# Elementwise products of a state-space table builder and a head norm from GpSimd to VectorE, and 1 / rms applied by ScalarE behind the rotary step

## The chip, the cores and the metric

The kernel runs on one core of one Trainium2 chip. The time is the device time of one execution in microseconds (us). The engines work side by side, each on its own queue of instructions in a fixed order: TensorE (PE in the rows; PEld is its weight load), VectorE (DVE), ScalarE (ACT), GpSimd (POOL) and SyncE (SP), which here only issues transfers. An instruction that waits holds up all that stand behind it on its engine.

## The reference, cut to what matters

One step of a hybrid decoder layer for a prompt of 512 tokens and for 8 single tokens that continue cached sequences. One input projection feeds a diagonal state-space group (S5) and an attention group with three branches; both are gated, concatenated and projected out. The change touches two pieces of it, the norm with rotary step of the heads, and the discretised tables of the state-space group:

```python
def rms_norm(x, w):
    y = xf * lax.rsqrt(jnp.mean(xf * xf, axis=-1, keepdims=True) + RMS_EPS)
    return (y * w).astype(x.dtype)

def rope(x, pos):                     # first 16 of 64 columns of a head
    return concatenate([x1 * cos - x2 * sin, x2 * cos + x1 * sin, rest], axis=-1)

q = rope(rms_norm(q.reshape(B, S, 8, 64), q_norm_w), pos)
ks = rope(rms_norm(kv[:, :, 0::2], k_norm_w), pos)      # 3 branches x 2 heads of keys

# s5_scan: h[t] = a * h[t-1] + B u[t], y = Re(C h) + D u, with a = exp(lam dt) complex
```

## The kernel before

All products of the dense projections are made as three TensorE passes (L121 to L123: high by high, high by low, low by high), so every weight block is split on the way in: ScalarE copies the high part (`whi`), VectorE subtracts it (`wlo`).

The program up to about 205 us of the trace merges two streams. `dense` makes the projections, block of 256 columns by block: keys and values, queries (tile `qraw`, evacuated from TensorE's accumulator `a` by ScalarE), then the four gate blocks (`gate_mm`, tile `sg`, evacuated by VectorE as `sg<-a` and by ScalarE as `sgS<-a`). `ssm_all` works the 32 state-space groups in four rounds `sq` of eight: `ssm_tables(sq)` builds the tables `P` (turned by TensorE and copied by ScalarE to `WX`), `WY`, `E` and the kernel `ktc`; `ssm_run(sq)` makes `Xc` on TensorE, turns it with `E` into `ga`, scans it on VectorE (`ga<-coef,ga`), and multiplies the result `HB` with `WY` (L782) and the input with `TT` (L787); ScalarE copies the sum out as `ga<-t`. `coef`, one buffer, is written by ScalarE for each scan and waits for the scan before.

`norm_rope(i, keys)` runs between the dense blocks for the four tiles of 128 prompt rows and for the 8 sample rows (`kvs`, `qsr`), once for keys and once for queries: ScalarE squares into `sq` (two buffers, shared), GpSimd multiplies the norm weight in, VectorE reduces (`rsq<-sq`) and scales, GpSimd raises to -1/2 (L168), VectorE multiplies 1 / rms in and does the rotary step (`ra`, `rb`, then back into the tile). Finished keys go out by SP's queue. Behind 205 us lie prompt attention, the gathered cache of the sample rows, the gated unit and the output projection.

The order of each engine's queue is made when the program is built, by a scheduler that walks the recorded program with estimated durations; reads from PSUM get a higher priority. So a change of engine also moves other instructions. The two calls that the change moves about are

```python
def rstd_of(out, ssq, n, parts, cols):
    V.tensor_scalar(out, ssq, 1.0 / n, EPS, op0=ALU.mult, op1=ALU.add)
    return G.tensor_tensor(out, out, mhalf[:parts, :cols], op=ALU.pow)
```

and, in `norm_rope`, the product of the whole tile with `rb`. L61 and L62 are the wrapper through which all VectorE and ScalarE calls go, so those rows are told apart by their tiles.

Of the kernel before, what the change touches and what calls it, by code (L numbers as in the profile page):

```python
# [13 lines left out]
ALU = mybir.AluOpType  # L14
# [22 lines left out]
def hymba_step_kernel(  # L37
# [9 lines left out]
    G, T = nc.gpsimd, nc.tensor  # L47
# [18 lines left out]
    V, S = PsumFirst(nc.vector), PsumFirst(nc.scalar)  # L66
# [16 lines left out]
    def pt_(name, cols=1024, dt=F32, parts=128):  # L83
        return big.tile([parts, cols], dt, tag="P", name=nm(name), bufs=NP)
# [7 lines left out]
    def st(shape, name, dt=F32, bufs=1, tag=None):  # L92
        n = nm(name)
        return sm.tile(shape, dt, tag=tag or n, name=n, bufs=bufs)

    def k2(name, cols=512, parts=128, dt=F32):
        return sm.tile([parts, cols], dt, tag="k2", name=nm(name), bufs=NK)
# [4 lines left out]
    def k1(name, cols=128, parts=128, dt=F32):  # L102
        return sm.tile([parts, cols], dt, tag="k1", name=nm(name), bufs=NS)
# [6 lines left out]
    def pb(use):  # L110
        tag = ROUTE[use]
        return psum.tile([128, 512], F32, tag=tag, name=nm(tag), bufs=BANKS[tag])
# [53 lines left out]
# [3 lines that stand above are left out]
# [102 lines left out]
    rs = st([8, 1], "rs")  # L271
# [172 lines left out]
    def rowset(i):  # L444
        if i < 4:
            return 128, kvt[i], qraw[i // 2][:, 512 * (i % 2):512 * (i % 2) + 512]
        return 8, kvs, qsr
# [63 lines left out]
    def part_of(n, w):  # L511
        j = 0 if so[0] + n * w <= HW else 1
        o = so[j]
        so[j] += n * w
        return ssm[j][:, o:o + n * w].rearrange("p (a b) -> p a b", b=w)
# [92 lines left out]
    pwr, pwi, pni = part_of(9, 16), part_of(9, 16), st([128, 9, 16], "pni", tag="pni")  # L608
# [15 lines left out]
    CTr, CTi, CNi = part_of(16, 16), part_of(16, 16), st([128, 16, 16], "CNi", tag="CNi")  # L624
# [14 lines left out]
    bbr, bbi = part_of(16, 16), part_of(16, 16)  # L639
# [28 lines left out]
    def ssm_tables(sq):  # L668

        gs = slice(4 * sq, 4 * sq + 4)  # L670
        P_ = pt_("P")
        Pr, Pi, pt1, pt2 = P_[:, 0:512], P_[:, 512:1024], k2("pt"), k2("pt")

        def v4(t):
            return t.rearrange("p (g s c) -> p g s c", s=8, c=16)

        def pw4(t, e0):
            return t[:, e0:e0 + 8, gs].rearrange("p e g -> p g e").unsqueeze(3).to_broadcast([128, 4, 8, 16])

        def c4(t):  # L680
            return t[:, gs].unsqueeze(2).to_broadcast([128, 4, 8, 16])

        V.tensor_tensor(v4(pt1), pw4(pwr, 1), c4(bbr), op=ALU.mult)
        G.tensor_tensor(v4(pt2), pw4(pni, 1), c4(bbi), op=ALU.mult)
        V.tensor_tensor(Pr, pt1, pt2, op=ALU.add)
        V.tensor_tensor(v4(pt1), pw4(pwr, 1), c4(bbi), op=ALU.mult)
        G.tensor_tensor(v4(pt2), pw4(pwi, 1), c4(bbr), op=ALU.mult)
        V.tensor_tensor(Pi, pt1, pt2, op=ALU.add)
        for g2 in range(2):
            sl = slice(64 * g2, 64 * g2 + 64)  # L690
            S.copy(cb[sl, 0, :, g2, :], CTr[sl, gs])
            S.copy(cb[sl, 1, :, g2, :], CNi[sl, gs])
        WX = pt_("WX")
        for a in range(2):
            p = pb("tr")
            for b in range(4):
                T.transpose(p[:, 128 * b:128 * b + 128], P_[:, 512 * a + 128 * b:512 * a + 128 * b + 128], ident)
            S.copy(WX[:, 512 * a:512 * a + 512], p)
        p = pb("tr")
        for a in range(2):  # L700
            for gp in range(4):
                T.matmul(p[32 * gp:32 * gp + 32, 0:128], cb[:, a, gp].rearrange("p a c -> p (a c)"),
                         P_[:, 512 * a + 128 * gp:512 * a + 128 * gp + 128], start=(a == 0), stop=(a == 1),
                         skip_group_check=True, tile_position=(0, 32 * gp))
        ktt = k1("ktt")
        S.copy(ktt, p[:, 0:128])
        p = pb("tr")
        T.transpose(p[:, 0:128], ktt, ident)

        ktc = k1("ktc")  # L710
        k3_ = ktc.rearrange("p (c g) -> p g c", g=8)
        S.copy(k3_, p[:, :128].rearrange("p (g c) -> p g c", c=16))
        V.tensor_tensor(k3_[96:128], k3_[96:128], Dm[96:128, 128 * sq:128 * sq + 128].rearrange("p (g c) -> p g c", c=16),
                        op=ALU.add)
        nc.sync.dma_start(scr_k[sq, 0:128, :], ktc)

        WY = pt_("WY")
        w1_, w2_ = k2("wt"), k2("wt")
        V.tensor_tensor(v4(w1_), pw4(pwr, 0), c4(CTr), op=ALU.mult)
        G.tensor_tensor(v4(w2_), pw4(pni, 0), c4(CTi), op=ALU.mult)  # L720
        V.tensor_tensor(WY[:, 0:512], w1_, w2_, op=ALU.add)
        V.tensor_tensor(v4(w1_), pw4(pni, 0), c4(CTr), op=ALU.mult)
        G.tensor_tensor(v4(w2_), pw4(pwr, 0), c4(CNi), op=ALU.mult)
        V.tensor_tensor(WY[:, 512:1024], w1_, w2_, op=ALU.add)

        E = k2("E").rearrange("p (a g k) -> p a g k", a=2, k=64)
        for a in range(2):
            S.copy(E[:, a, :, 0:32], UW[a][:, gs, 0:32])
        es = k2("es").rearrange("p (b a g k) -> p b a g k", b=2, a=2, k=32)
        for b in range(2):  # L730
            V.tensor_tensor(es[:, b], E[:, :, :, 0:32], UW[b][:, gs, 32:33].unsqueeze(1).to_broadcast([128, 2, 4, 32]), op=ALU.mult)
        V.tensor_tensor(E[:, 0, :, 32:64], es[:, 0, 0], es[:, 1, 1], op=ALU.subtract)
        V.tensor_tensor(E[:, 1, :, 32:64], es[:, 0, 1], es[:, 1, 0], op=ALU.add)
        return WX, WY, E
# [85 lines left out]
    def norm_rope(i, keys):  # L820

        n, kv_, q_ = rowset(i)
        if keys:
            src = kv_.rearrange("p (k v n) -> p k v n", v=2, n=128)[:, :, 0, :]
            hd, h, sh = src.rearrange("p k (g d) -> p k g d", g=2), 6, (n, 3, 2)
            nw_ = nw4[:n, 1:4].unsqueeze(2).to_broadcast([n, 3, 2, 64])
            e = lambda t: t.rearrange("p (k g) d -> p k g d", g=2)
            bc = lambda t: t.unsqueeze(1).unsqueeze(1).to_broadcast([n, 3, 2, 8])
        else:
            src = q_  # L830
            hd, h, sh = src.rearrange("p (h d) -> p h d", d=64), 8, (n, 8)
            nw_ = nw4[:n, 0:1].to_broadcast([n, 8, 64])
            e = lambda t: t
            bc = lambda t: t.unsqueeze(1).to_broadcast([n, 8, 8])
        sq = k3("sq", 64 * h, n)
        S.activation(sq.rearrange("p (k n) -> p k n", n=128) if keys else sq, src, AF.Square)
        G.tensor_tensor(hd, hd, nw_, op=ALU.mult)
        rs = st([n, 14], "rsq", bufs=2, tag=f"rsq{n}")[:, 0:h]
        V.tensor_reduce(rs, sq.rearrange("p (h d) -> p h d", d=64), axis=AX.X, op=ALU.add)
        o = C_ROPE + 16 * i if i < 4 else C_ROPS  # L840
        cos, sin = bc(cst[:n, o:o + 8]), bc(cst[:n, o + 8:o + 16])
        x1, x2 = hd[..., 0:8], hd[..., 8:16]
        rstd_of(rs, rs, 64, n, h)
        rb = e(rs.unsqueeze(2)) if keys else rs.unsqueeze(2)
        V.tensor_tensor(hd, hd, rb.to_broadcast([*sh, 64]), op=ALU.mult)
        ra, rb_ = k1("ra", 128, n), k1("rb", 128, n)
        r_ = [e(t[:, 8 * h * j:8 * h * j + 8 * h].rearrange("p (h d) -> p h d", d=8)) for t in (ra, rb_) for j in range(2)]
        for out, x, cs_ in zip(r_, (x1, x2, x2, x1), (cos, sin, cos, sin)):
            V.tensor_tensor(out, x, cs_, op=ALU.mult)
        V.tensor_tensor(x1, r_[0], r_[1], op=ALU.subtract)  # L850
        last["nr"] = V.tensor_tensor(x2, r_[2], r_[3], op=ALU.add)
        if not keys:
            return
        if i < 4:
            nc.sync.dma_start(kvp_rows[128 * i:128 * i + 128], kv_[:, 0:512])
            nc.sync.dma_start(winp_rows[128 * i:128 * i + 128], kv_[:, 512:768])
        else:
            nc.sync.dma_start(kv_sample[0, :, 0].rearrange("b k g d -> b (k g d)"), kvs[:, 0:512])
            nc.sync.dma_start(win_sample[0, :, 511].rearrange("b k g d -> b (k g d)"), kvs[:, 512:768])
# [49 lines left out]
    def dense():  # L909
# [19 lines left out]
        for i in (4, 0, 1):  # L929
            norm_rope(i, True)  # L930
# [816 lines left out]
```

## Time and profile before

| | before |
|---|---|
| median of 3 runs | 485.32 us (484.53 to 486.43) |
| the profiled execution | 485.31 us |
| its span in the trace | 483.4 us |
| TensorE busy | 456.5 us, 94% of the span |
| VectorE busy | 353.8 us, 73% |
| ScalarE busy | 241.1 us, 50% |
| GpSimd busy | 124.8 us, 26% |

The span is the stretch from the first to the last instruction in the trace; the time has 1.9 us more around it. Busy shares are means over stages that differ. Matmuls overlap in the rows, so a busy TensorE is one that has something in flight.

### The profile page before, as it was taken

How to read it: one execution, taken by the hardware profiler on the slowest of the kernel's cores; microseconds unless marked ns; L12 is line 12 of the kernel's file. 1: busy time of each engine (PE TensorE's matmuls, PEld its weight loads, DVE VectorE, ACT ScalarE, POOL GpSimd, SP SyncE). 2: the span in 40 equal slices, each digit the busy share in tenths (PEclk: the TensorE clock that was granted, in tenths of full speed). 3: DMA queues.
4: the chain of work that ended last, by engine and by line, in shares of the span. 5: the costliest groups of instructions: out<-in, count | busy, mean ns of one | idle time of the engine just before them, and what ended most of it. 6: DMA issues, size and time to landing. Idle time of an engine off the chain costs nothing.

```text
span 483.4 us, 10948 instructions
## 1 busy us (share of the span) xinstructions
PE 456.5 (94%) x4258; PEld 387.9 (80%) x4258; DVE 353.8 (73%) x914; ACT 241.1 (50%) x585; POOL 124.8 (26%) x130
## 2 busy tenths in 40 slices
PE   7999999889698999979999999999999899999997
PEld 4989998688697898979867866777667599899886
DVE  6978999999998974648485875868557667774332
ACT  5914755545234222656675667747565636442100
POOL 3100045489673000063244213421324010000000
PEclk8999999899899999989999999999999899999999
DMA  8776622335256182065433272337244974612211
GB/s 285 234 218 169 112 52 89 92 91 115 48 144 191 51 195 39 1 216 177 133 102 117 88 263 88 129 122 241 92 161 132 261 179 132 173 35 77 66 45 46
DMA packets 75603, 62.84 MB, mean 130 GB/s; under 512 B 29230, under 2 KB 69024, under 8 KB 75424
## 3 DMA queue, kind: packets, MB, share of 16 engines
q1 hardware_dynamic: 66176, 36.74, 27.8%
q0 software_dynamic: 4816, 17.03, 10.7%
q10 hardware_dynamic: 4560, 8.39, 5.6%
q8 instruction: 33, 0.54, 0.5%
q14 instruction: 18, 0.15, 0.1%
HBM read 55.63 MB, written 10.70 MB: 137 GB/s over the span
## 4 chain that ended last, share of the span: by engine, by line
PE 65%; DVE 19%; issue 8%; DMA 5%; ACT 2%; POOL 1%; SPq 0%; DVEq 0%; POOLq 0%; ACTq 0%
PE a L121 9%; PE a L122 9%; PE a L123 9%; PE ph L1362 8%; PE a L1252 4%; PE a L1216 4%; PE t L1243 3%; DVE wlo L62 3%; PE t L1338 3%; DVE ga L62 3%; PE c L1535 2%; DMA kvg<-in_cache_kv_dram,idx 2%; PE t L1328 2%; DVE rsq L62 1%; DMA x<-in_x_prompt_dram 1%
## 5 line engine op out<-in xcount | busy, mean ns | idle before, releaser
L121 PE MATMUL a<-hTh,whi 128*128 128x256 f32 (+1 forms) x192 | 55.6, 291 | 7.3 <-ACT qraw L61 4.4
L122 PE MATMUL a<-hTh,wlo 128*128 128x256 f32 (+1 forms) x192 | 55.4, 290 | 0.0
L1319 POOL DMA_INDIRECT kvg<-in_cache_kv_dram,idx x32 | 31.9, 998 | 89.0 <-PE c L1119 56.1
L123 PE MATMUL a<-hTl,whi 128*128 128x256 f32 (+1 forms) x192 | 53.9, 287 | 0.0
L123 PE MATMUL a<-wlo,hTh 128*128 128x256 f32 (+1 forms) x160 | 46.6, 292 | 2.3 <-DVE wlo L62 2.3
L121 PE MATMUL a<-whi,hTh 128*128 128x256 f32 (+1 forms) x160 | 46.3, 293 | 0.0
L122 PE MATMUL a<-whi,hTl 128*128 128x256 f32 (+1 forms) x160 | 46.1, 289 | 0.0
L1362 PE MATMUL ph<-XT,W1h 128*128 128x256 f32 x256 | 44.7, 298 | 0.2 <-ACT XT L61 0.2
L121 PEld LDWEIGHTS a<-hTh,whi 128*128 128x128 f32 x192 | 36.9, 192 | 8.7 <-ACT qraw L61 4.6
L61 ACT ACTIVATE P<-a,mx 128x128 f32<-128x128 f32 (+3 forms) x64 | 33.6, 533 | 13.4 <-DVE mx L61 12.1
L61 DVE TENSOR_REDUCE mx<-a 128x1 f32<-128x384 f32 (+3 forms) x48 | 28.0, 596 | 13.5 <-PE a L1217 13.4
L122 PEld LDWEIGHTS a<-hTh,wlo 128*128 128x128 f32 x192 | 36.9, 192 | 0.6 <-issue 0.4
L123 PEld LDWEIGHTS a<-hTl,whi 128*128 128x128 f32 x192 | 36.4, 192 | 0.0
L121 PE MATMUL a<-woh,mixh 128*128 128x256 f32 x128 | 36.2, 285 | 0.0
L123 PE MATMUL a<-wol,mixh 128*128 128x256 f32 x128 | 36.1, 284 | 0.0
L122 PE MATMUL a<-woh,mixl 128*128 128x256 f32 x128 | 35.8, 282 | 0.0
L1362 PEld LDWEIGHTS ph<-XT,W1h 128*128 128x128 f32 x256 | 34.8, 190 | 1.0 <-ACT XT L61 0.6
L123 PEld LDWEIGHTS a<-wlo,hTh 128*128 128x128 f32 x160 | 31.0, 194 | 2.9 <-DVE wlo L62 2.5
L1322 POOL COPY Vs<-kvg 128x256 f32<-128x256 f32 x32 | 14.5, 454 | 70.2 <-DMA kvg<-in_cache_kv_dram,idx 47.7
L121 PEld LDWEIGHTS a<-whi,hTh 128*128 128x128 f32 x160 | 30.7, 194 | 1.1 <-issue 0.6
L122 PEld LDWEIGHTS a<-whi,hTl 128*128 128x128 f32 x160 | 30.8, 193 | 0.9 <-issue 0.9
L61 ACT COPY pT<-t 128x512 f32<-128x512 f32 x40 | 22.9, 587 | 12.9 <-PE t L1243 10.1
(412 smaller groups left out, 1272.1 us busy)
## 6 DMA issues: line engine op xcount, KB each, us to landing
w<-in_w_in_dram SPq DMA_DIRECT2D x16, 512.0 KB
out_dram<-in_cache_win_dram ACTq DMA_DIRECT2D x8, 511.0 KB
x<-in_x_prompt_dram SPq DMA_DIRECT2D x4, 512.0 KB
TT<-scr_k SPq DMA_DIRECT2D x4, 512.0 KB
w<-in_w_in_dram SPq DMA_DIRECT2D x16, 128.0 KB
W1r<-in_cmp_w_dram SPq DMA_DIRECT2D x4, 512.0 KB
wk<-in_cache_win_dram SPq DMA_DIRECT2D x8, 256.0 KB
wv<-in_cache_win_dram SPq DMA_DIRECT2D x8, 256.0 KB
```

Source lines behind the costliest of these rows:

```text
L61: return f(*args, **kw)
L62: return f(*args, **kw)
L121: T.matmul(out, ah, bh, start=start, stop=False, skip_group_check=True)
L122: T.matmul(out, al, bh, start=False, stop=False, skip_group_check=True)
L123: T.matmul(out, ah, bl, start=False, stop=stop, skip_group_check=True)
L1216: T.matmul(bank, QTv(g, r)[:, qsl], KTv(g, a)[:, brs, :n], start=(a == 0), stop=False, skip_group_check=True)
L1243: T.transpose(p[:, 128 * r:128 * r + 128], P[r][:, br, 128 * kt:128 * kt + 128], ident)
L1252: mm = T.matmul(po[64 * br:64 * br + 64, :], kvt[kt - 1][:, c0:c0 + 64], behind[kt - 1][br][0], start=(kt == 1), stop=(kt == i + 1), tile_ ...
L1319: G.indirect_dma_start(out=gt_, out_offset=None, in_=ckv, in_offset=bass.IndirectOffsetOnAxis(ap=idx[:, 2 * pr_ + b2, jq:jq + 1], axis=0))
L1322: G.tensor_copy(Vs[b2][:, 2 * jq:2 * jq + 2, :], gf[:, :, 384:512])
L1338: T.transpose(p[:, 256 * g + 128 * b2:256 * g + 128 * b2 + 128], gts[jq][b2][:, o:o + 128], ident)
L1362: T.matmul(ph3[:, kd], (W1l if part == 1 else W1h)[kd][a][:, wsl], (xl if part == 2 else xh)[:, e, a:a + 256], start=(jq == 0 and kd == 0 ...
```

## The change

The four products on GpSimd in `ssm_tables` (16 in the whole program) and the norm weight product in `norm_rope` (10) become VectorE instructions. The VectorE product of a tile with 1 / rms (10) is removed; in its place ScalarE multiplies each head, 64 columns, by its own row scale, in place: 6 copies for a tile of keys, 8 for a tile of queries, 70 in all. They stand behind the rotary step, which now works on heads that are not yet divided by their rms. GpSimd keeps the power -1/2.

```diff
         V.tensor_tensor(v4(pt1), pw4(pwr, 1), c4(bbr), op=ALU.mult)
-        G.tensor_tensor(v4(pt2), pw4(pni, 1), c4(bbi), op=ALU.mult)
+        V.tensor_tensor(v4(pt2), pw4(pni, 1), c4(bbi), op=ALU.mult)
         V.tensor_tensor(Pr, pt1, pt2, op=ALU.add)
         V.tensor_tensor(v4(pt1), pw4(pwr, 1), c4(bbi), op=ALU.mult)
-        G.tensor_tensor(v4(pt2), pw4(pwi, 1), c4(bbr), op=ALU.mult)
+        V.tensor_tensor(v4(pt2), pw4(pwi, 1), c4(bbr), op=ALU.mult)
...
-        G.tensor_tensor(v4(w2_), pw4(pni, 0), c4(CTi), op=ALU.mult)
+        V.tensor_tensor(v4(w2_), pw4(pni, 0), c4(CTi), op=ALU.mult)
...
-        G.tensor_tensor(v4(w2_), pw4(pwr, 0), c4(CNi), op=ALU.mult)
+        V.tensor_tensor(v4(w2_), pw4(pwr, 0), c4(CNi), op=ALU.mult)
...
-        G.tensor_tensor(hd, hd, nw_, op=ALU.mult)
+        V.tensor_tensor(hd, hd, nw_, op=ALU.mult)
         rs = st([n, 14], "rsq", bufs=2, tag=f"rsq{n}")[:, 0:h]
         V.tensor_reduce(rs, sq.rearrange("p (h d) -> p h d", d=64), axis=AX.X, op=ALU.add)
...
-        rstd_of(rs, rs, 64, n, h)
-        rb = e(rs.unsqueeze(2)) if keys else rs.unsqueeze(2)
-        V.tensor_tensor(hd, hd, rb.to_broadcast([*sh, 64]), op=ALU.mult)
         ra, rb_ = k1("ra", 128, n), k1("rb", 128, n)
...
         last["nr"] = V.tensor_tensor(x2, r_[2], r_[3], op=ALU.add)
+        rstd_of(rs, rs, 64, n, h)
+        for j in range(h):
+            o = (256 * (j // 2) + 64 * (j % 2)) if keys else 64 * j
+            s_ = (kv_ if keys else q_)[:, o:o + 64]
+            S.mul(s_, s_, rs[:, j:j + 1])
```

The scheduler makes new queues of it. VectorE's, where the tables of the first two rounds begin (`pt` and `wt` are the two factors' products, `P` and `WY` their sums; the second product of each pair was GpSimd's), before:

```order
L62 TENSOR_TENSOR pt_624<-ssm_325,ssm_326 128x512
L62 TENSOR_TENSOR ssm_325<-ssm_325 128x64
L62 TENSOR_SCALAR pni_411<-ssm_325 128x144
L62 TENSOR_TENSOR wt_667<-ssm_325 128x512
L62 TENSOR_TENSOR es_678<-E_675,UW_380 128x256
L62 TENSOR_TENSOR es_678<-E_675,UW_381 128x256
L62 TENSOR_TENSOR pt_865<-ssm_325,ssm_326 128x512
L62 TENSOR_TENSOR P_623<-pt_624,pt_625 128x512
```

and in the changed program:

```order
L62 TENSOR_TENSOR pt_624<-ssm_325,ssm_326 128x512
L62 TENSOR_TENSOR ssm_325<-ssm_325 128x64
L62 TENSOR_SCALAR pni_411<-ssm_325 128x144
L62 TENSOR_TENSOR pt_625<-pni_411,ssm_326 128x512
L62 TENSOR_TENSOR wt_667<-ssm_325 128x512
L62 TENSOR_TENSOR wt_668<-pni_411,ssm_326 128x512
L62 TENSOR_TENSOR P_623<-pt_624,pt_625 128x512
L62 TENSOR_TENSOR es_678<-E_675,UW_380 128x256
```

`pt_625` and `wt_668` are now made on the same queue, and the first sum `P` no longer waits for another engine.

ScalarE's queue in the third round, from the split of a gate block on (`coef` is the buffer that waits for the scan before it), before:

```order
L62 CAST whi_1796<-w_1790 128x1024
L61 ACTIVATE qraw_315<-a_1701,rsd_122 128x256
L62 COPY ssm_326<-ssm_325 64x4x16 x2
L61 COPY ktt_1332<-t_1323 128x128
L62 COPY ssm_326<-CNi_438 64x4x16 x2
L61 COPY ktc_1336<-t_1334 128x8x16
L61 ACTIVATE qraw_314<-a_1960,rsd_122 128x256
L62 ACTIVATE sq_2212<-qraw_314 128x512
L61 ACTIVATE qraw_315<-a_2011,rsd_122 128x256
L62 COPY coef_482<-ssm_325 128x4x63
L61 ACTIVATE qraw_314<-a_1960,rsd_122 128x256
```

and in the changed program:

```order
L62 CAST whi_2095<-w_2089 128x1024
L61 ACTIVATE qraw_315<-a_2036,rsd_122 128x256
L62 COPY ssm_326<-ssm_325 64x4x16 x2
L61 COPY ktt_1332<-t_1323 128x128
L62 COPY ssm_326<-CNi_438 64x4x16 x2
L61 COPY ktc_1336<-t_1334 128x8x16
L62 COPY coef_482<-ssm_325 128x4x63
L62 CAST whi_2236<-w_2226 128x1024
```

All eight evacuations `qraw<-a` now stand ahead of this `coef`; before, some stood behind it.

A little further on the same queue (`ga<-t` empties the two banks into which TensorE puts its next transposes), before:

```order
L61 COPY Xc_1861<-c_1862 128x288
L61 COPY Xc_1861<-c_1872 128x288
L62 ACTIVATE sq_2482<-qraw_315 128x512
L62 COPY hfin_486<-HB_1584 128x2x4
L62 COPY hs_485<-Xc_1861 128x16x4
L62 COPY HB_1894<-h_470 128x8x9
L61 COPY ga_1572<-t_1590 128x4x72
L61 COPY ga_1572<-t_1591 128x4x72
```

and in the changed program:

```order
L61 COPY sgS_494<-a_2123 128x8
L62 ACTIVATE kvs<-kvs,rsq_1499 8x64 x6
L61 COPY Xc_1886<-c_1887 128x288
L61 COPY Xc_1886<-c_1897 128x288
L62 CAST whi_2240<-w_2231 128x1024
L62 COPY hfin_486<-HB_1599 128x2x4
L62 COPY hs_485<-Xc_1886 128x16x4
L62 ACTIVATE kvt_309<-kvt_309,rsq_1522 128x64 x6
L61 COPY sgS_494<-a_2174 128x8
L62 ACTIVATE kvt_310<-kvt_310,rsq_1545 128x64 x6
L62 COPY HB_1919<-h_470 128x8x9
L61 COPY ga_1587<-t_1605 128x4x72
```

Two trains of six copies, each waiting for its tile's rotary step and power, now stand ahead of that evacuation. On TensorE's queue the last round's products L782 and L787 stand later among the dense passes: fewer passes of the last gate block are left behind them than before. From the attention on, TensorE's queue is the same.

## Rows read from the trace of the kernel before

**Rows 1.** The page: busy us, share of the span and instructions of each engine.

```profile
PE 456.5 (94%) x4258; PEld 387.9 (80%) x4258; DVE 353.8 (73%) x914; ACT 241.1 (50%) x585; POOL 124.8 (26%) x130
```

**Rows 2.** Busy time by stage; PEclk is TensorE's granted clock, 1.00 its upper level.

```profile
core 0: us, PE busy (x) PEld busy (x) DVE busy (x) ACT busy (x) POOL busy (x), PEclk, DMA share, GB/s
62.00:105.00 43.00, 40.68 (x445) 36.50 (x445) 41.82 (x71) 21.81 (x55) 22.48 (x15) 0.96 0.32 90
105.00:153.00 48.00, 38.97 (x436) 36.61 (x435) 45.06 (x91) 21.23 (x50) 36.45 (x22) 0.96 0.45 111
153.00:177.00 24.00, 21.96 (x306) 20.85 (x304) 22.62 (x79) 4.23 (x11) 0.00 (x0) 1.00 0.45 116
177.00:205.50 28.50, 27.41 (x320) 26.56 (x320) 15.91 (x43) 13.78 (x38) 0.00 (x0) 1.00 0.23 48
205.50:483.00 277.50, 268.45 (x2300) 215.82 (x2296) 176.23 (x440) 144.62 (x363) 59.98 (x80) 0.99 0.43 134
```

**Rows 3.** TensorE's waits between 60 and 206 us: us in total, times, longest.

```profile
PE a L121 <- ACT qraw L61: 4.4, 1, 4.4
PE a L121 <- DVE sg L61: 2.9, 3, 1.4
PE a L123 <- DVE wlo L62: 2.3, 1, 2.3
PE t L702 <- ACT WX L61: 1.9, 2, 1.1
PE t L697 <- ACT ga L61: 1.8, 1, 1.8
PE t L782 <- DVE HB L62: 0.7, 1, 0.7
```

**Rows 4.** Two short windows with TensorE's granted clock, columns as in rows 2.

```profile
92.80:96.20 3.40, 3.37 (x15) 3.37 (x16) 3.40 (x5) 3.31 (x9) 1.94 (x1) 0.51 0.57 154
130.30:133.70 3.40, 3.40 (x18) 3.40 (x18) 3.40 (x14) 3.21 (x7) 2.95 (x1) 0.52 0.07 14
```

**Rows 5.** ScalarE in order of time: start, us, engine, line, operation, shapes, idle before.

```profile
129.24 0.40 ACT L62 COPY coef<-ssm 128x252 f32<-128x252 f32 x1 [9.11 <-DVE ga L62]
129.54 0.47 ACT L61 ACTIVATE qraw<-a,rsd 128x256 f32<-128x256 f32 x1
```

**Rows 6.** GpSimd in order of time: a table product, and a power.

```profile
83.31 1.56 POOL L723 TENSOR_TENSOR wt<-ssm,CNi 128x512 f32<-128x512 f32 x1 [3.82 <-DVE WY L62]
...
107.05 1.78 POOL L168 TENSOR_TENSOR rsq<-rsq,mhalf 128x6 f32<-128x6 f32 x1
```

**Rows 7.** VectorE in order of time.

```profile
65.04 1.75 DVE L62 TENSOR_TENSOR es<-E,UW 128x256 f32<-128x256 f32 x2 [0.76 <-ACT E L62]
...
70.82 0.68 DVE L62 TENSOR_TENSOR pt<-ssm,ssm 128x512 f32<-128x512 f32 x1
71.42 0.68 DVE L62 TENSOR_TENSOR wt<-ssm 128x512 f32<-128x512 f32 x1
...
80.57 0.75 DVE L62 TENSOR_TENSOR es<-E,UW 128x256 f32<-128x256 f32 x2
...
83.81 1.61 DVE L62 TENSOR_TENSOR ga<-Xc,E 128x512 f32<-128x512 f32 x1
...
107.55 0.67 DVE L62 TENSOR_TENSOR pt<-ssm,ssm 128x512 f32<-128x512 f32 x1
...
138.06 1.84 DVE L62 TENSOR_TENSOR es<-E,UW 128x256 f32<-128x256 f32 x2
```

**Rows 8.** The VectorE products with 1 / rms; duration ns min/median/max, first and last start.

```profile
L62 DVE TENSOR_TENSOR kvt<-kvt,rsq x4: 528/540/1358, 108.9 to 129.1; 128x384 f32<-128x384 f32 x4
L62 DVE TENSOR_TENSOR qraw<-qraw,rsq x4: 675/677/693, 142.6 to 150.9; 128x512 f32<-128x512 f32 x4
```

**Rows 9.** Two neighbouring ScalarE instructions on 64 columns with a row operand, columns as rows 8.

```profile
L61 ACT ACTIVATE gx<-c,hb x2: 306/310/313, 209.1 to 209.3; 128x64 f32<-128x64 f32 x2
```

**Rows 10.** GpSimd's first gather of the cache.

```profile
205.55 1.13 POOL L1319 DMA_INDIRECT kvg<-in_cache_kv_dram,idx  x1 [55.08 <-PE c L1119]
```

## The prediction

> **What bounds the kernel now.** I read the busy shares first: TensorE has something in flight for 94% of the span, VectorE for 73%, ScalarE for half, GpSimd for a quarter [rows 1]. By those averages no work on VectorE matters. So I read the stages next [rows 2]. Behind 205.5 us TensorE is busy for 268.45 of 277.5 us and the change touches nothing there. But from 62 to 153 us, where all tables and norms lie, VectorE is busy for 41.82 of 43.00 and 45.06 of 48.00 us: it has no gap to speak of, and TensorE has. In the middle stage TensorE is at 38.97 of 48.00. Then the picture turns: from 177 us VectorE is down to 15.91 of 28.5 us, and TensorE works almost without a gap through dense passes that were left over, until GpSimd's first gather starts at 205.55, having waited 55.08 us for TensorE's L1119 [rows 10]. So whatever TensorE loses between 62 and 205.5 us pushes the gather and the whole rest back by as much, and that loss is the stake.
>
> What it loses: its waits between 60 and 206 us come to 4.4 + 2.9 + 2.3 + 1.9 + 1.8 + 0.7 = 14.0 us [rows 3]. Behind the two longest (2.3 us for `wlo`, 4.4 us for the evacuation of `qraw`) the granted clock stands at 0.51 and 0.52, the lower of its two levels, for 3.4 us [rows 4]; at half rate each of those stretches loses about 1.7 us. Together 14.0 + 3.4 = 17.4 us is all that can be won there.
>
> Who makes TensorE wait? `wlo` and `HB` are VectorE's. The 4.4 us are told by ScalarE's own row: `coef` waits 9.11 us for VectorE's scan of the round before, and the evacuation of `qraw` stands right behind it, at 129.54 [rows 5]. The waits for `ga` and `WX` are evacuations too; ScalarE was behind squares whose buffers VectorE had not yet reduced. So 11.1 of the 14.0 us (all but 2.9 for `sg`) are VectorE being late, directly or through ScalarE's queue.
>
> **The change part by part.** *VectorE gets 16 table products.* The nearest rows are its own halves of the same pairs: 0.68 us long, and the next starts 0.60 us later (70.82, 71.42) [rows 7]. 16 x 0.60 = 9.6 us more.
>
> *VectorE gets 10 weight products and loses 10 products with 1 / rms.* Same tiles, two inputs each: 0.54 and 0.68 us a piece for full tiles [rows 8]. I take them as equal: 0. If the weight operand, which is repeated over heads in another pattern, made them a tenth dearer, that is 0.6 us; a tenth cheaper gives that back.
>
> *GpSimd no longer runs 26 products beside VectorE.* Here is the larger term, and the mean durations hide it. At 83.31 GpSimd starts a table product of 1.56 us; VectorE's `ga<-Xc` that starts at 83.81 takes 1.61 us, where a product of that size takes 0.68 [rows 6, 7]. The pair `es` takes 0.75 us for two at 80.57, and 1.75 and 1.84 at 65.04 and 138.06 [rows 7]. I went through all VectorE rows from 62 to 153 us and took those at least 0.3 us longer than the usual row of their shape: 20 rows, the first at 65.04, the last at 138.06, each while a product that the change removes was running on GpSimd, most of them 0.9 us too long; the excess sums to 19.1 us. The powers that stay on GpSimd do no such thing: during the one at 107.05 a product of two inputs takes its 0.67 us [rows 6, 7]. So I count all 19.1 us as given back. From below: if half of the excess were something else, 9.5 us.
>
> VectorE's sum: +9.6 + 0 - 19.1 = -9.5 us, between 0 (half of the excess) and -9.5. It would do more instructions in less time.
>
> *ScalarE gets 70 copies of 64 columns.* The trace has no such row with SBUF at both ends. The nearest is a pair of ACTIVATEs on 64 columns with a row operand, 0.31 us each, the second starting 0.2 us behind the first [rows 9]. I take 0.21 us, in trains of 6 or 8: 70 x 0.21 = 14.7 us; from above 70 x 0.31 = 21.7 us; from below nothing, where a train falls into an idle stretch. Between 62 and 205.5 us ScalarE is busy for 61.05 of 143.5 us [rows 2], so there is room for all. Uncovered, they would cost their own 14.7 us less the 5 or so that VectorE's products took, and the clock on top.
>
> The row prices a tile of queries at 8 x 0.21 = 1.7 us on ScalarE where VectorE took 0.68 [rows 8]. The Trainium skill, "ScalarE: Activation LUTs", speaks against this edit: under "Rules for kernel authors" it says of multiplications to use VectorE, not ScalarE. Its section "What ACT_TABLE_LOAD costs" gives 186 ns, 93 for a row operand and 0.833 a column, less 93 of overlap: an estimate of 239 ns, so 16.7 us for 70; with that in place of 14.7 the ScalarE load is 2 us more and the sum below the same, as long as ScalarE has its idle time.
>
> The copies also put a wait on ScalarE's queue: each train waits for its tile's rotary step on VectorE and for the power on GpSimd. Behind the trains of the keys stand `HB` and the two `ga<-t`, which empty the banks for TensorE's next transposes; behind the last trains of the queries, the copies `qs` of the attention. SP's stores of finished keys come later too, and weights that stand behind them on SP; these are wanted only by the compression, in the stretch behind 177 us, so I price this at 0 (if that cover is gone, it shows as TensorE waiting at the first L1119).
>
> *Where the waits go.* In the new order the splits `wlo` of the query block stand some 10 us of VectorE work earlier, and with 7 us of excess gone before 90 us too, the 2.3 us go. All `qraw` evacuations are ahead of that `coef`: the 4.4 us go. `WX`, `ga` and `HB` (1.9 + 1.8 + 0.7) go because VectorE reaches its reductions and sums sooner, while TensorE's queue asks for them later. That is 11.1 us, and the two clock stretches follow: 3.4. I keep the 2.9 us for `sg`. As a new wait I charge one train pair of twelve copies in front of an evacuation, 12 x 0.21 = 2.5 us, since at least one such place will not fit.
>
> Sum, against the profiled execution's 485.31 us (whose span is 1.9 us shorter, and which agrees with the median of 485.32): 485.3 - 11.1 - 3.4 + 2.5 = 473.3 us.
>
> **The rivals.** *Copies on the path.* ScalarE does in 14.7 us what took VectorE about 6, on a queue that also empties TensorE's banks. If all that difference reached TensorE, 8.7 us: 485.3 - 14.5 + 8.7 = 479.5. For it: ScalarE's waits reach TensorE today [rows 5]. Against: its idle half. The skill's rule named above (products belong on VectorE) would bring this case.
>
> *VectorE stays the pace.* If TensorE simply follows VectorE, only VectorE's net counts, 485.3 - 9.5 = 475.8, and with half of the excess 485.3, no change. For the latter: the dense passes left over behind 177 us could have hidden any delay. Against: a delay of TensorE is never hidden, since it runs through to the gather.
>
> *Trains that stop ScalarE: slower.* Each train waits for VectorE and GpSimd in turn. One stop of 9.11 us today cost TensorE 4.4 us and 1.7 of clock, 6.1 in all [rows 3 to 5]. The 14.5 us won pay for 2.4 such stops; from the third on the kernel is slower: 485.3 - 14.5 + 18.3 = 489.1. For it: ten trains, and the scheduler that placed them didn't know VectorE's excess (it placed an evacuation behind a 9 us wait). Against: that excess is just what goes, and rotary steps end well ahead of most trains.
>
> *All of it.* Every wait goes, `sg` too: 485.3 - 17.4 = 467.9.
>
> **How the numbers follow.** The likeliest case, 473.3, gets 0.52 (its own range 469 to 478); everything won, below 469, 0.12; copies on the path or VectorE's net, 478 to 482.9, 0.20; no change within 0.5%, which is about what this measurement can tell apart (482.9 to 487.7), 0.09; stopped trains, 0.07. The range from 466 to 482 leaves out the last two, and a few in a hundred on either side. Faster 0.84, same 0.09, slower 0.07.
>
> **What the profile after would show.** Right: `es`, `ga<-Xc`, `WY`, `pt` at 0.37 to 0.68 us throughout, none at 1.6; VectorE with gaps between 62 and 160 us; no `coef` row that waits 9 us with a `qraw` behind it; no lower clock near 92 and 130 us; the copies at about 0.3 us, 0.2 apart; the first gather at about 193 instead of 205.55, and the rest as long as before, 277 us. Wrong: rows of VectorE still stretched, beside the powers; or TensorE waiting for `ga`, `WX` or `sg` behind trains of copies; or the first L1119 waiting for late weights.

## The result, and the profile after

The changed kernel takes 472.37 us (median of 4 runs, 472.14 to 473.57) where the kernel before took 484.92 us (4 runs, 482.19 to 486.43): a ratio of 0.9753, 95% interval 0.9719 to 0.9787. The profiled execution after took 472.14 us with a span of 470.3 us.

The page of the changed kernel, busy us, share of the span and instructions of each engine:

```profile
PE 453.0 (96%) x4258; PEld 386.2 (82%) x4258; DVE 343.6 (73%) x930; ACT 258.0 (55%) x655; POOL 89.8 (19%) x104
```

Against [rows 1], VectorE runs 16 instructions more and is busy 10.2 us less. ScalarE gained 16.9 us, and GpSimd lost 35.0.

Busy time of the changed kernel by stage, columns as in [rows 2]; the last two stages are divided where the gather now starts:

```profile
62.00:105.00 43.00, 43.00 (x412) 39.39 (x411) 41.73 (x81) 24.48 (x57) 6.18 (x2) 1.00 0.38 102
105.00:153.00 48.00, 46.28 (x587) 44.66 (x587) 40.88 (x110) 27.68 (x80) 12.62 (x6) 1.00 0.49 126
153.00:177.00 24.00, 23.09 (x325) 22.30 (x324) 20.97 (x71) 12.81 (x47) 4.62 (x3) 1.00 0.41 104
177.00:194.00 17.00, 14.57 (x199) 13.38 (x198) 11.39 (x37) 12.25 (x37) 0.77 (x1) 0.80 0.13 25
194.00:470.00 276.00, 266.11 (x2271) 214.48 (x2267) 175.83 (x437) 144.60 (x361) 59.83 (x80) 0.99 0.44 135
```

In the two stages in which the tables are built TensorE goes from 40.68 and 38.97 us to 43.00 and 46.28 (with 412 matmuls in the first where 445 stood before, and 587 in the second where there were 436), and its clock no longer falls there. VectorE's gaps stay as they were in the first stage and grow from 3 to 7 us in the second.

TensorE's waits between 60 and 200 us in the changed kernel, columns as in [rows 3]:

```profile
PE t L1330 <- DMA kvg<-in_cache_kv_dram,idx: 2.1, 1, 2.1
PE t L708 <- ACT ktt L61: 1.7, 1, 1.7
PE a L1004 <- DVE sg L61: 1.7, 1, 1.7
PE a L121 <- DVE sg L61: 0.9, 1, 0.9
PE c L1278 <- DVE KN L61: 0.4, 1, 0.4
PE t L810 <- ACT ga L61: 0.3, 1, 0.3
```

The first line is behind the gather and belongs to the part that the change leaves alone. The other five come to 5.0 us, where [rows 3] came to 14.0 (14.2 with a wait of 0.2 us for `ktt` that is not among its lines). The first gather, in order of time:

```profile
193.24 1.09 POOL L1321 DMA_INDIRECT kvg<-in_cache_kv_dram,idx  x1 [18.57 <-PE c L1121]
```

It stood at 205.55 [rows 10], 12.3 us later; from there to the end it is 277.1 us (before 277.9). Two groups of instructions by tile show how much of this one execution's lead has nothing to do with the change; the first start (after "first and last start") of the first dense matmul, before:

```profile
L121 PE MATMUL a<-hTh,whi x192: 276/282/469, 11.2 to 197.5; 128*128 128x256 f32 x96, 128*128 128x264 f32 x96
```

and in the changed kernel:

```profile
L121 PE MATMUL a<-hTh,whi x192: 276/283/464, 9.9 to 180.1; 128*128 128x256 f32 x96, 128*128 128x264 f32 x96
```

The projections start 1.3 us earlier. In all profiled executions of this study that start lies between 9.7 and 12.1 us, whatever the kernel, so a single pair of traces carries an error of this size before the change has begun.

VectorE of the changed kernel in order of time, at the places of [rows 7]:

```profile
63.34 0.68 DVE L62 TENSOR_TENSOR wt<-ssm 128x512 f32<-128x512 f32 x1
63.94 0.69 DVE L62 TENSOR_TENSOR wt<-pni,ssm 128x512 f32<-128x512 f32 x1
65.14 0.75 DVE L62 TENSOR_TENSOR es<-E,UW 128x256 f32<-128x256 f32 x2
...
83.37 0.69 DVE L62 TENSOR_TENSOR ga<-Xc,E 128x512 f32<-128x512 f32 x1
```

The second half of a pair (`wt<-pni,ssm`, formerly GpSimd's) costs 0.60 us behind the first, `es` is back from 1.75 to 0.75, `ga<-Xc` from 1.61 to 0.69. None of the rows from 62 to 177 us is 0.3 us longer than its shape's usual one.

ScalarE's copies, grouped by tile, columns as in [rows 8]:

```profile
L62 ACT ACTIVATE qraw<-qraw,rsq x32: 331/333/352, 163.1 to 178.6; 128x64 f32<-128x64 f32 x32
L62 ACT ACTIVATE kvt<-kvt,rsq x24: 331/334/352, 131.2 to 145.4; 128x64 f32<-128x64 f32 x24
```

Each is 0.33 us long. A train of six takes 1.55 us, so they follow each other at (1.55 - 0.33) / 5 = 0.24 us.

What new wait there is comes together at one place. All engines of the changed kernel in order of time, from 136.5 to 146 us:

```profile
137.00 8.57 POOL L168 TENSOR_TENSOR rsq<-rsq,mhalf 128x6 f32<-128x6 f32 x3 [29.48 <-ACT sq L62]
...
140.22 0.67 DVE L62 TENSOR_TENSOR wt<-pni,ssm 128x512 f32<-128x512 f32 x1
140.82 0.67 DVE L62 TENSOR_TENSOR wt<-ssm,CNi 128x512 f32<-128x512 f32 x1
142.69 0.71 DVE L62 TENSOR_TENSOR ga<-Xc,E 128x512 f32<-128x512 f32 x1 [1.19 <-DMA scr_y<-ga]
142.72 2.50 ACT L62 ACTIVATE kvt<-kvt,rsq 128x64 f32<-128x64 f32 x10 [3.90 <-POOL rsq L168]
...
145.65 0.25 ACT L61 COPY ktt<-t 128x128 f32<-128x128 f32 x1
...
145.95 0.33 PE L708 MATMUL t<-cst,ktt 128*128 128x128 f32 x1 [1.72 <-ACT ktt L61]
```

A power on GpSimd, 1.3 to 3.4 us elsewhere in this kernel and 1.3 to 2.5 in the kernel before, lasts 5.7 us here (the longest of its group; three of them are one row of 8.57). It ends within VectorE's first gap: VectorE is dense until 141.5. The train of copies had waited 3.90 us for it, the evacuation `ktt` stands behind the two trains in ScalarE's queue, and TensorE waits 1.72 us for `ktt`.

Last, the granted clock of the changed kernel in four short windows, columns as in [rows 2]:

```profile
177.00:181.00 4.00, 3.65 (x33) 3.28 (x31) 1.19 (x4) 4.00 (x12) 0.00 (x0) 1.00 0.10 16
181.00:185.00 4.00, 1.92 (x30) 1.60 (x28) 3.97 (x11) 2.46 (x8) 0.00 (x0) 0.86 0.37 71
185.00:189.00 4.00, 4.00 (x29) 3.77 (x29) 2.30 (x13) 3.08 (x13) 0.00 (x0) 0.50 0.06 16
189.00:193.20 4.20, 4.20 (x87) 3.94 (x88) 3.93 (x12) 2.71 (x9) 0.00 (x0) 0.79 0.02 4
```

The two stretches at the lower level of [rows 4] are gone, but one of about 7 us stands behind the waits for `sg` (1.7) and `KN` (0.4), where there was none before.

### The profile page after: what moved, and what is told of

It is laid out like the page before. It is cut to its first block, busy times and chain, and to the rows that moved or that the text cites. A ratio compares the mean times of both kernels' runs of the same rounds, so it can differ in the third digit from the quotient of the medians.

```text
span 470.3 us, 11016 instructions
## 1 busy us (share of the span) xinstructions
PE 453.0 (96%) x4258; PEld 386.2 (82%) x4258; DVE 343.6 (73%) x930; ACT 258.0 (55%) x655; POOL 89.8 (19%) x104
## 4 chain that ended last, share of the span: by engine, by line
PE 68%; DVE 11%; DMA 7%; issue 7%; ACT 3%; POOL 2%; SPq 1%; POOLq 0%; DVEq 0%; ACTq 0%
PE a L121 11%; PE a L122 11%; PE a L123 10%; PE ph L1364 8%; PE a L1218 3%; DMA kvg<-in_cache_kv_dram,idx 3%; PE a L1254 3%; PE t L1245 3%; PE c L1537 2%; PE t L1340 2%; DVE ga L62 2%; PE t L1330 1%; PE ph L473 1%; DVE wlo L62 1%; POOL rsq L168 1%
## 5 line engine op out<-in xcount | busy, mean ns | idle before, releaser
L121 PE MATMUL a<-hTh,whi 128*128 128x256 f32 (+1 forms) x192 | 54.8, 286 | 0.9 <-DVE sg L61 0.9
L168 POOL TENSOR_TENSOR rsq<-rsq,mhalf 128x6 f32<-128x6 f32 (+3 forms) x10 | 23.4, 2348 | 131.3 <-DVE rsq L62 83.0
L123 PE MATMUL a<-wlo,hTh 128*128 128x256 f32 (+1 forms) x160 | 45.3, 284 | 0.0
L121 PE MATMUL a<-whi,hTh 128*128 128x256 f32 (+1 forms) x160 | 45.2, 287 | 0.0
L61 ACT ACTIVATE P<-a,mx 128x128 f32<-128x128 f32 (+3 forms) x64 | 33.6, 534 | 14.0 <-DVE mx L61 12.3
L121 PEld LDWEIGHTS a<-hTh,whi 128*128 128x128 f32 x192 | 36.2, 188 | 1.5 <-DVE sg L61 1.1
L121 PE MATMUL a<-woh,mixh 128*128 128x256 f32 x128 | 36.1, 284 | 0.0
L121 PEld LDWEIGHTS a<-whi,hTh 128*128 128x128 f32 x160 | 29.8, 188 | 0.9 <-issue 0.4
```

The costliest lines, as they stand in the source:

```text
L61: return f(*args, **kw)
L121: T.matmul(out, ah, bh, start=start, stop=False, skip_group_check=True)
L123: T.matmul(out, ah, bl, start=False, stop=stop, skip_group_check=True)
```

## The experiments

Each was timed in several rounds against the kernel before on the same chip; a ratio is to that. "Waits" are TensorE's between 60 us and its first gather, added up as above, as far as the profile puts them down to another engine.

| kernel | median us | ratio, 95% interval | waits us |
|---|---|---|---|
| before | 484.92 | 1 | 14.2 |
| the change | 472.37 | 0.9753 (0.9719 to 0.9787) | 5.0 |
| the change again (e10_after) | 472.30 | 0.9735 (0.9700 to 0.9770) | 4.0 |
| table products alone (e1_tables) | 482.60 | 0.9979 (0.9942 to 1.0016) | 10.1 |
| weight products alone (e2_weights) | 479.49 | 0.9899 (0.9871 to 0.9928) | 7.3 |
| ScalarE copies alone (e3_copies) | 483.02 | 0.9980 (0.9916 to 1.0045) | 14.2 |
| both kinds of products (e4_products) | 469.42 | 0.9695 (0.9628 to 0.9763) | 1.6 |
| the same again (e11_products) | 470.18 | 0.9690 (0.9650 to 0.9730) | 1.6 |
| the change, 1 / rms on VectorE, same place (e7_scale_v) | 472.94 | 0.9788 (0.9728 to 0.9848) | 4.2 |
| the change, copies ahead of the rotary step (e9_copies_ahead) | 468.57 | 0.9660 (0.9625 to 0.9695) | 3.1 |
| the change, GpSimd products beside (e5_beside) | 478.34 | 0.9883 (0.9837 to 0.9929) | 8.4 |
| the change, memsets early (e5c_memset) | 474.33 | 0.9816 (0.9769 to 0.9863) | 4.6 |
| the change, memsets beside (e12_memset_beside) | 472.67 | 0.9740 (0.9695 to 0.9786) | 5.1 |
| the change, one-input copies beside (e13_read_beside) | 485.31 | 1.0024 (1.0001 to 1.0048) | 16.4 |

**Is it GpSimd that stretched VectorE?** My theory was that VectorE's rows were long because GpSimd ran products beside them; the rival, that the order of the queues made the gain. This kernel adds GpSimd work, into a scratch tile that nobody reads, to the changed kernel; the other four queues stay as they are.

```diff
         V.tensor_tensor(v4(pt2), pw4(pni, 1), c4(bbi), op=ALU.mult)
+        for q in range(4):
+            G.tensor_tensor(gs4, pw4(pni, 1)[:, q:q + 1], c4(bbi)[:, q:q + 1], op=ALU.mult)
```

(and so behind the other three).

> The changed kernel, with sixteen times four GpSimd products of 128 columns (two SBUF inputs, into a scratch tile that nobody reads) added beside the sixteen VectorE table products. The queues of TensorE, VectorE, ScalarE and SyncE are word for word those of the changed kernel. Theory of contention: VectorE rows are stretched again while such a product runs, about 11 us in all (the share of the 19.1 us that the table products had), and TensorE waits return in part: about 478, 475 to 482 us. Rival, the new order made the gain and the contention is harmless: 472.4 us, as the changed kernel.

It came out 6 us above the change. VectorE and GpSimd of this kernel in order of time:

```profile
62.89 0.69 DVE L62 TENSOR_TENSOR pt<-pni,ssm 128x512 f32<-128x512 f32 x1
62.95 3.39 POOL L689 TENSOR_TENSOR gscr<-pni,ssm 128x128 f32<-128x128 f32 x4 [43.11 <-DVE pni L62]
63.50 0.91 DVE L62 TENSOR_TENSOR wt<-ssm 128x512 f32<-128x512 f32 x1
64.33 0.90 DVE L62 TENSOR_TENSOR wt<-pni,ssm 128x512 f32<-128x512 f32 x1
...
72.32 5.45 POOL L734 TENSOR_TENSOR gscr<-ssm,CNi 128x128 f32<-128x128 f32 x4
73.69 0.67 DVE L62 TENSOR_TENSOR WY<-wt,wt 128x512 f32<-128x512 f32 x1
```

VectorE's rows go from 0.69 to 0.90 us as soon as GpSimd starts, and its busy time from 62 to 177 us from 103.6 to 111.9 us. Not every row is stretched: `WY` at 73.69 keeps its 0.67 us, and there it is GpSimd's four products that last 5.45 us instead of about 3. The same queue of VectorE is slower only because of what runs on GpSimd.

The powers come later in this kernel too (the first at 128.2 us instead of 95.2), since they queue behind the products. But ScalarE's waits for powers come to 4.4 us between 85 and 185 us, fewer than the 5.9 of the change, while its waits for VectorE's scans and reductions (`coef`, `sq`) go from 4.2 to 15.3 us. This speaks for VectorE as the way by which the loss comes.

It gives back 6 of the 12.5 us, and not all. VectorE is as busy as in the kernel before over the whole span (353.2 against 353.8 us), and still the kernel is 1.2% faster. What the other half is made of (the new order of the queues, or the removed collisions with the weight products) no run separates.

**Does the mere work on GpSimd do it, or its reading?** A first control put memsets in place of the products (`G.memset(gs4, 0.0)`).

> As the run with products beside, but GpSimd writes zeros of the same 128 columns, 64 times, and reads nothing. Theory that it is GpSimd's reading of SBUF that holds VectorE up: no stretched rows, 472.4 us. Rival, any GpSimd instruction does: stretched rows and a time like that of the run with products.

It missed its place: memsets wait for nothing, and in its trace all 64 ran between 3.5 and 28 us, ahead of the tables. It says only that so many more instructions cost little there. So two more kernels first copy one column of the table just used, which holds the rest back until VectorE is there, and then do eight memsets, or eight copies of a constant:

```diff
         V.tensor_tensor(v4(pt2), pw4(pni, 1), c4(bbi), op=ALU.mult)
+        G.tensor_copy(gscr[:, 0:1], pni[:, 1, 4 * sq:4 * sq + 1])
+        for q in range(8):
+            G.memset(gscr, 0.0)                      # e12_memset_beside
+            G.tensor_copy(gscr, cst[:, 0:128])       # e13_read_beside, instead
```

> As the change, with extra GpSimd work at the places of the 16 table products: first a copy of one column of the table just used (so that the work starts beside VectorE's products and not before them), then eight memsets of 128 columns. The other engines' queues are those of the change. The memsets write but read nothing. If what stretches VectorE is GpSimd reading SBUF: es, pt and ga<-Xc at their plain 0.68 to 0.75 us beside the memsets, 472 to 474.5 us. If any GpSimd activity stretches it (or its load alone, through the powers that queue behind): as the extra products did, 477 to 479.5 us, rows of 0.9 us.

> The same with eight copies of 128 columns of a constant instead of the memsets: one input read, one output written, none of the tiles that VectorE works on. If reading is what counts: products of VectorE at about 0.9 us beside them, 475 to 479 us. If only operations of two inputs, or tiles shared with VectorE, do it: as the changed kernel, 472 to 474.5 us.

With memsets, VectorE and GpSimd in order of time:

```profile
66.31 0.68 DVE L62 TENSOR_TENSOR wt<-ssm 128x512 f32<-128x512 f32 x1
66.49 2.05 POOL L689 MEMSET gscr<- 128x128 f32 x8
66.91 0.68 DVE L62 TENSOR_TENSOR wt<-pni,ssm 128x512 f32<-128x512 f32 x1
```

GpSimd is busy for 60.3 us of the 115 us from 62 to 177, more than twice the 23.4 of the change, right beside VectorE's products, and these take their 0.68 us; the time is that of the change. So activity alone does nothing.

The copies, which read one input, made the kernel as slow as before, but not by the way I expected. VectorE's rows went only from 0.69 to 0.77 us. It was GpSimd that suffered. GpSimd, ScalarE and TensorE of that kernel in order of time:

```profile
137.31 7.81 POOL L695 COPY gscr<-cst 128x128 f32<-128x128 f32 x8
...
145.43 2.78 POOL L731 COPY gscr<-cst 128x128 f32<-128x128 f32 x8
...
151.87 2.61 POOL L168 TENSOR_TENSOR rsq<-rsq,mhalf 128x6 f32<-128x6 f32 x2
153.23 1.54 ACT L62 ACTIVATE kvt<-kvt,rsq 128x64 f32<-128x64 f32 x6 [13.15 <-POOL rsq L168]
...
156.16 0.24 ACT L61 COPY ktt<-t 128x128 f32<-128x128 f32 x1
...
156.46 0.48 PE L716 MATMUL t<-cst,ktt 128*128 128x128 f32 x1 [12.35 <-ACT ktt L61]
```

Eight copies take 2.78 us while VectorE waits and 7.81 while it runs products. The powers stand behind them and are late, the train of copies on ScalarE waits 13.15 us, and `ktt` behind the train makes TensorE wait 12.35 us: nearly the whole loss of 13 us in one place. Of my two cases for this run neither held: reading on GpSimd does collide, but the price was paid by GpSimd's queue and what waits for it.

**Which part makes the gain?** One part alone each, on the kernel before.

Table products alone:

```diff
-        G.tensor_tensor(v4(pt2), pw4(pni, 1), c4(bbi), op=ALU.mult)
+        V.tensor_tensor(v4(pt2), pw4(pni, 1), c4(bbi), op=ALU.mult)
```

(four such lines).

> The kernel before with only the sixteen table products on VectorE; weights stay on GpSimd, 1 / rms on VectorE. Theory of contention: VectorE gets 9.6 us of work and is rid of about 11 us of stretching, -1.6 us net, while the order changes: about 480, 476 to 484 us. Rival, the copies on ScalarE made the gain by taking work from VectorE: no faster than before, 485 us or more.

Weight products alone:

```diff
-        G.tensor_tensor(hd, hd, nw_, op=ALU.mult)
+        V.tensor_tensor(hd, hd, nw_, op=ALU.mult)
```

> The kernel before with only the ten norm weight products on VectorE. Theory of contention: VectorE gets 5.4 us and is rid of about 8 us of stretching: about 482, 478 to 485 us. Rival, only the table products matter: 485 us.

Copies alone, with all products left on GpSimd:

```diff
-        rstd_of(rs, rs, 64, n, h)
...
-        V.tensor_tensor(hd, hd, rb.to_broadcast([*sh, 64]), op=ALU.mult)
...
+        rstd_of(rs, rs, 64, n, h)
+        for j in range(h):
...
+            S.mul(s_, s_, rs[:, j:j + 1])
```

> The kernel before with only the 1 / rms part changed: 70 ScalarE copies behind the rotary step, all 26 products still on GpSimd. Theory of contention: VectorE loses 5.4 us of work but keeps 19 us of stretching: about 480, 476 to 484 us. Rival, the copies made the gain: 473 us. Rival, copies in front of evacuations cost more than they give: above 485 us.

Both kinds of products (the two edits above together), with 1 / rms on VectorE as before.

> All 26 products on VectorE, 1 / rms on VectorE ahead of the rotary step as before, no ScalarE copies. Theory of contention: VectorE gets 15.0 us and is rid of 19.1: -4 us net, about 477, 473 to 481 us, above the changed kernel by what the copies are worth. Rival, the copies made the gain: 485 us.

The parts don't add. The tables alone bring 0.2% with an interval over 1, the weights alone 1.0%, together 5.9 us; both at once bring 3.1%, 15 us. TensorE's waits with the tables alone:

```profile
PE a L121 <- ACT sgS L61: 4.2, 1, 4.2
PE t L708 <- ACT ktt L61: 2.5, 1, 2.5
PE a L1002 <- DVE sg L61: 2.2, 1, 2.2
PE t L697 <- ACT ga L61: 1.2, 1, 1.2
```

The waits of [rows 3] for `wlo`, `qraw` and `WX` are gone, others have come: VectorE, with 9.6 us more to do, got back only 8 and is still stretched, mostly by the weights' products, and ScalarE is late for `sgS` instead. Counted by the prediction's rule (rows at least 0.3 us over their shape's usual one, each instruction by itself), the excess is about 19.5 us before (19.1 in the prediction), 11.4 in e1_tables, 12 in e2_weights, 19.5 in e3_copies, and none in the change and in e4_products. The copies alone leave 14.2 us of waits too, and the time as it was.

e3_copies and e4_products also show that it is not VectorE's load that counts: it is busy for 348.5 and 348.4 us in them, and they are 13.6 us apart.

Not all of the excess lies beside products. VectorE and GpSimd of e3_copies in order of time, at a place where only the powers run on GpSimd:

```profile
132.96 5.68 POOL L168 TENSOR_TENSOR rsq<-rsq,mhalf 128x6 f32<-128x6 f32 x3
135.37 1.77 DVE L62 TENSOR_TENSOR WY<-wt,wt 128x512 f32<-128x512 f32 x1
```

`WY` takes 0.67 us elsewhere. So a power can stretch a product of VectorE too.

Only when no product is left on GpSimd do the waits close; in e4_products two remain before the gather:

```profile
PE a L995 <- DVE qs L62: 1.1, 1, 1.1
PE a L121 <- DVE sg L61: 0.5, 1, 0.5
```

I had put e1_tables and e3_copies too low by 2.6 and 3.0 us, e2_weights too high by 2.5, and e4_products too high by 8, outside its range (473 to 481).

**Do the ScalarE copies bring or cost?** e4_products is faster than the change, which has the copies on top. Either the engine costs, or the place behind the rotary step. One kernel keeps the place and gives the product back to VectorE; the other keeps the copies and puts them ahead:

```diff
-        for j in range(h):                                                # e7_scale_v
...
-            S.mul(s_, s_, rs[:, j:j + 1])
...
+        V.tensor_tensor(hd, hd, rb.to_broadcast([*sh, 64]), op=ALU.mult)
```

> The changed kernel with 1 / rms on VectorE (10 products) behind the rotary step in place of the 70 ScalarE copies. Theory: VectorE has 5.4 us more than in the changed kernel, where it still waited for about 10 us between 60 and 175 us, so most of it is covered: about 474, 471 to 478 us. If the copies hold up ScalarE's evacuations, it is faster than the changed kernel: 471 us.

```diff
+        rstd_of(rs, rs, 64, n, h)                                         # e9_copies_ahead
+        for j in range(h):
...
+            S.mul(s_, s_, rs[:, j:j + 1])
         ra, rb_ = k1("ra", 128, n), k1("rb", 128, n)
```

(and the same lines taken out behind).

> As the change, but the power and the 70 ScalarE copies stand ahead of the rotary step, where 1 / rms was before. Theory A (only the place counts: behind the rotary step costs, the engine doesn't): about as fast as the two kinds of products alone, 469 to 471 us. Theory B (place is nothing, and a ScalarE train costs more than one VectorE product): 472 to 475 us; and since VectorE's rotary step now waits for ScalarE in the middle of its own run, possibly slower than the change: rows ra<-kvt with a wait for ACT rsq of 1 us or more.

On the same chip as this last one, the change and the two products again:

> The changed kernel as it is, on the same chip as the next one, to compare the two directly. Both theories: 472.4 us (471.5 to 473.5).

> The two kinds of products on VectorE and 1 / rms on VectorE ahead of the rotary step, as in the run of 469.42 us, once more beside the changed kernel. If the move of 1 / rms to ScalarE costs the time that the first runs suggest: 468.5 to 470.5 us, 2 to 4 us under the changed kernel, whole intervals apart. If that was chance: within 1 us of it.

Behind the rotary step: 472.4 and 472.3 by ScalarE, 472.9 by VectorE. Ahead of it: 468.6 by ScalarE, 469.4 and 470.2 by VectorE. So the engine makes no difference that these runs show, and the place makes 2 to 4 us. For the copies the intervals are apart (0.9625 to 0.9695 against 0.9700 to 0.9770); for VectorE's products ahead (0.9650 to 0.9730) they still overlap with the change on that chip. Behind, each kernel has one wait of 1.7 to 4.0 us on ScalarE's evacuations; e7_scale_v's longest is

```profile
PE t L810 <- ACT ga L61: 4.0, 1, 4.0
```

and e9_copies_ahead, of which the profile caught the longest run (472.77 us), has 1.0 for `ktt`. That the waits differ is shown; why the queues made with the step ahead fit better is not settled. Both e9_copies_ahead and e4_products beat the kernel before; e9_copies_ahead beats the change too, while the interval of e4_products (0.9628 to 0.9763) overlaps with the change's.

## Why the prediction was right

The forecast was 473.3 us; 472.37 came, inside the likeliest case's own range and in the main for the reasons given. One term did not hold, and one came out right only in sum.

- *VectorE, -9.5 us of work.* Right: 353.8 to 343.6 is -10.2. The 16 products cost 0.60 us each, as priced, and the whole excess of 19.1 us went. That GpSimd's reading beside VectorE stretches its rows is shown by e5_beside and e12_memset_beside; that this makes the gain is shown for about half of it (6 of 12.5 us). The Trainium skill, "SBUF — State Buffer", section "Who interferes with whom", says that a VectorE instruction with two SBUF inputs contends with a GpSimd instruction that reads SBUF and not with one that only writes; these two runs agree (0.90 against 0.68 us).
- *"The powers that stay on GpSimd do no such thing."* Read from one instance, and not so in general: in e3_copies `WY` took 1.77 us beside powers alone. In the changed kernel no row of VectorE is stretched, but there a power lasts 5.7 us beside VectorE's closed-up products. That these products are what held it up is the likely reading and was not tested by a run of its own. This is where the change loses 1.7 us again.
- *ScalarE's copies at 0.21 us, 14.7 in all.* Too low: 0.24, and 16.9 us more on ScalarE. The estimate from the Trainium skill, "ScalarE: Activation LUTs", section "What ACT_TABLE_LOAD costs", of 239 ns and 16.7 us was the better one; the length that its figures give for one copy, an estimate of 186 + 93 + 64 x 0.833 = 332 ns, is met by the rows too. As forecast it did not matter.
- *Waits: 11.1 recovered, 2.9 for `sg` kept, 2.5 new.* Right for the 11.1: all that were named are gone. 5.4 was forecast to be left and 5.0 is, but the split is luck. Of `sg` at L121, 2.9 us before, 0.9 is left, and 4.1 are new: 1.7 for `ktt` behind trains of copies (the prediction's own sign of being wrong, though small), 0.3 for `ga`, and 1.7 for `sg` and 0.4 for `KN` at other matmuls (L1004, L1278) at 182 to 184 us.
- *3.4 us from the clock.* The step that failed: "the two clock stretches follow". They went, and another of about 7 us came at 182 us, behind waits of 1.7 and 0.4 us in a passage that had been fully fed. It takes (1 - 0.86) x 4 + (1 - 0.50) x 4 + (1 - 0.79) x 4.2 = 3.4 us at most, so the term is nearer 0 than 3.4.
- *Why the sum still fits.* The profiled executions differ by 485.31 - 472.14 = 13.2 us: 9.2 from the waits (14.2 - 5.0), up to 1.3 from the earlier start, 0.8 behind the gather; about 2 are left that I cannot place (gaps too short for the list, and ends of matmuls that are modelled). The forecast's 12.0 had 3.4 of clock where chance and these remainders stand.
- *The rivals.* Copies on the path, 479.5: no, e7_scale_v without them is not faster. VectorE's pace, 475.8: no; in e4_products VectorE's busy time falls by only 5.4 us, and the gain is 15. Stopped trains: the mechanism exists. In the change a stop of 3.90 us costs 1.7; in e13_read_beside one of 13.15 us cost 12.35. The prediction priced a stop of 9.11 us at 6.1, two thirds of it, and a long one can cost nearly the whole. In the change nothing long stands ahead of the powers on GpSimd; that this kept the stops short is argued from e13_read_beside.

## What to carry to other kernels

Look for the longest instance of an instruction, not its mean: rows of one shape that are 0.9 us too long only while another engine runs are work that can be won twice, once where they run and once where others wait for them. Such collisions are best taken away whole: with a part of them left in place the waits moved to other tiles, and the two parts brought 1.0 and 4.9 us where both together brought 15. And when an engine closes its gaps, ask which small operation on the neighbour lived in those gaps, and who stands in the queue behind whoever waits for it.

## What the runs showed of the hardware

- The collision goes both ways, and which side pays differs: beside GpSimd's products of 128 x 512 VectorE lost 0.9 us a row, beside its products of 128 x 128 0.22, beside its one-input copies of 128 x 128 only 0.08, while those copies went from 0.35 us each (8 in 2.78) to 0.98 (8 in 7.81). Beside memsets of 0.21 us neither lost anything. Where GpSimd's products of 128 x 128 met rows of VectorE that kept their 0.67 us, four of them lasted 5.45 us.
- A power on six columns, which reads almost nothing, lasted up to 5.7 us beside a closed run of VectorE's instructions and ended within VectorE's first gap (6.05 us in e4_products). Beside powers alone a product of VectorE took 1.77 us instead of 0.67. The spans of GpSimd are rough in a profile, but ScalarE's 3.90 us of waiting for it are not.
- A wait of 1.7 us at 144 us left TensorE's granted clock at its upper level in the changed kernel (1.00 in that whole stage), and waits of 1.7 and 0.4 us that ended at 183.3 and 184.2 us were followed by the lower one. In e4_products too the clock is at 0.70 over the stage from 177 to 194 us, with only one wait of 1.1 us near it.
